# Batch norm over 64 tiles: loads and stores issued in turn from one ring of three buffers, in place of phases of three stores and three loads

## The chip, the cores and the metric

The kernel runs on one core of one Trainium2 chip. The metric is the device time of one execution in microseconds (us). A profiled execution also has a span, the time from its first to its last recorded event, which is about 1.8 us shorter. All runs named here are of the fast state; none fell into the slower state that some executions show. Where a ratio is given, it is the mean time of one kernel's fast runs over the mean of the other's fast runs of the same rounds, so it is not quite the ratio of the medians that stand beside it.

## The reference

```python
# x: (32, 256, 128, 128) float32; the parameters have 256 values, one for each channel
gamma * (x - running_mean) / np.sqrt(running_var + 1e-5) + beta
```

This is one multiplication and one addition for each element, with a scale and a shift that depend on the channel only. The input has 536.87 MB and so has the output. There is nothing to reuse, so the kernel is a stream: read everything, change it, write everything.

## The kernel before

The 32 x 256 channel planes are viewed as 64 tiles of 128 partitions by 16384 columns, 8.39 MB each, one contiguous row of 64 KB for each partition. Three such tiles fit the pool. All loads and stores go through the DMA queue of SP, the engine that issues them, in program order. DVE, the vector engine, does the arithmetic.

```python
NBUF = 3
GROUPS = [3] * 20 + [2, 2]
...
    def load(i):
        t = data.tile([P, HW], f32, tag="t")          # one of NBUF buffers in turn
        nc.sync.dma_start(out=t[:], in_=xr[i])
        tiles[i] = t
...
    def compute(i): ...                                # DVE, in place: t = t * scale + shift
    def store(i):
        t = tiles.pop(i)
        nc.sync.dma_start(out=outr[i], in_=t[:])
...
    first = 0
    for g, size in enumerate(GROUPS):
        idxs = range(first, first + size)
        for i in idxs:
            compute(i)
        for i in idxs:
            store(i)
        first += size
        more = GROUPS[g + 1] if g + 1 < len(GROUPS) else 0
        for i in range(first + AHEAD, min(first + AHEAD + more, NT)):   # AHEAD is 0
            load(i)
```

The framework puts in the waits: a compute waits for its load to land, a store for its compute, and a load for the store that frees its buffer.

## Time and profile before

| | before |
|---|---|
| time, median of the first 3 runs | 2487.11 us (2486.21 to 2487.93) |
| span of the profiled run | 2483.6 us |
| DVE busy | 566.0 us, 23% |
| share of the 16 DMA engines' time that the one data queue fills | 99.9% |
| mean rate | 432 GB/s |
| one load or store of a tile, in the steady part | 19.35 us |

The row to read first is the DMA engines' share. DVE is idle for three quarters of the span, but idle time of an engine that isn't the bound costs nothing. The lines themselves stand in the prediction.

### The profile page before, as it was taken

The numbers are of one execution on the slowest core, as the hardware profiler recorded it, in microseconds if no ns is written. First come the engines' busy times: TensorE is split into PE (matmuls) and PEld (weight loads), VectorE is DVE, ScalarE is ACT, GpSimd is POOL, SyncE is SP. The second block draws the span as 40 slices with busy tenths as digits, with TensorE's granted clock in tenths as the row PEclk, the third lists the DMA queues.
The fourth block names the chain that finished last, engine by engine and source line by source line (L and its number), as shares of the span: only waits on it lengthen the run. The fifth ranks groups of instructions, "written<-read, shape, count | busy, mean of one in ns | idle before, by whom it ended". The sixth has DMA issues, their size and how long they took to land.

```text
span 2483.6 us, 383 instructions
## 1 busy us (share of the span) xinstructions
DVE 566.0 (23%) x75; ACT 1.6 (0%) x2; POOL 0.2 (0%) x4
## 2 busy tenths in 40 slices
DVE  3140404121221213140403121221213040403112
ACT  0000000000000000000000000000000000000000
POOL 0000000000000000000000000000000000000000
DMA  9999999999999999999999999999999999999999
GB/s 421 423 439 439 425 436 439 431 431 439 431 431 439 435 426 436 436 431 435 435 435 427 439 434 427 439 434 427 439 437 432 432 437 433 431 437 433 431 437 396
DMA packets 18442, 1073.77 MB, mean 432 GB/s; under 512 B 2052, under 2 KB 2056, under 8 KB 2056
## 3 DMA queue, kind: packets, MB, share of 16 engines
q1 hardware_dynamic: 18432, 1073.75, 99.9%
q14 instruction: 2, 0.02, 0.0%
q10 hardware_dynamic: 8, 0.00, 0.0%
HBM read 536.88 MB, written 536.87 MB: 432 GB/s over the span
## 4 chain that ended last, share of the span: by engine, by line
another core or an unknown queue 72%; DVE 22%; DMA 4%; issue 0%; DVEq 0%; SPq 0%
DVE t L93 22%; DMA t<-in_x_dram 4%; DVEq L93 0%; SPq L51 0%; SPq L104 0%
## 5 line engine op out<-in xcount | busy, mean ns | idle before, releaser
L93 DVE TENSOR_SCALAR t<-t,scale_t,shift_t 128x16384 f32<-128x16384 f32 x64 | 564.0, 8812 | 1863.9 <-DMA t<-in_x_dram 1863.8
L66 DVE STREAM_TRANSPOSE turned<-rows 32x256 f32<-32x256 f32 x1 | 0.4, 432 | 21.5 <-DMA rows<-in_running_mean_dram 21.5
L78 ACT ACT_TABLE_LOAD x1 | 1.3, 1283 | 2.6 <-issue 2.6
L71 DVE COPY par<-turned 32x8 f32<-32x8 f32 x4 | 0.6, 161 | 0.1
L56 DVE MEMSET rows<- 32x256 f32 x1 | 0.3, 272 | 0.8 <-PEq L132 0.8
L78 ACT ACTIVATE tmp_t<-par,eps_t 128x2 f32<-128x2 f32 x1 | 0.3, 297 | 20.0 <-DVE par L71 20.0
L85 DVE RECIPROCAL tmp_t<-tmp_t 128x2 f32<-128x2 f32 x1 | 0.2, 165 | 0.4 <-ACT tmp_t L78 0.4
L87 DVE TENSOR_TENSOR tmp_t<-par,scale_t 128x2 f32<-128x2 f32 x1 | 0.2, 161 | 0.0
L88 DVE TENSOR_TENSOR shift_t<-par,tmp_t 128x2 f32<-128x2 f32 x1 | 0.2, 161 | 0.0
L86 DVE TENSOR_TENSOR scale_t<-par,tmp_t 128x2 f32<-128x2 f32 x1 | 0.2, 160 | 0.0
L132 POOL MEMSET const-uint8-127<- 128x1 uint8 x1 | 0.1, 103 | 0.0
L132 POOL MEMSET const-bfloat16-1.0<- 128x1 bf16 x1 | 0.1, 101 | 0.0
L132 POOL MEMSET const-float32-0.0<- 128x1 f32 x1 | 0.1, 98 | 0.2 <-issue 0.2
L132 POOL MEMSET const-float32-1.0<- 128x1 f32 x1 | 0.1, 98 | 0.0
L64 DVE MEMSET eps_t<- 128x1 f32 x1 | 0.1, 59 | 0.0
## 6 DMA issues: line engine op xcount, KB each, us to landing
t<-in_x_dram SPq DMA_DIRECT2D x64, 58.0
out_dram<-t SPq DMA_DIRECT2D x64, 49.1
rows<-in_running_var_dram ACTq DMA_DIRECT2D x1, 1.0 KB
rows<-in_gamma_dram ACTq DMA_DIRECT2D x1, 1.0 KB
rows<-in_beta_dram ACTq DMA_DIRECT2D x1, 1.0 KB
rows<-in_running_mean_dram ACTq DMA_DIRECT2D x1, 1.0 KB
```

The costliest lines, as they stand in the source:

```text
L56: nc.vector.memset(rows, 0.0)
L64: nc.vector.memset(eps_t, eps)
L66: nc.vector.transpose(out=turned[:], in_=rows[:])
L71: nc.vector.tensor_copy(out=par[q * B : (q + 1) * B], in_=blocks[:, :, q, 0:4])
L78: nc.scalar.activation(out=tmp_t[:], in_=var_t, func=mybir.ActivationFunctionType.Sqrt, bias=eps_t[:], scale=1.0,)
L85: nc.vector.reciprocal(out=tmp_t[:], in_=tmp_t[:])
L86: nc.vector.tensor_mul(out=scale_t[:], in0=gamma_t, in1=tmp_t[:])
L87: nc.vector.tensor_mul(out=tmp_t[:], in0=mean_t, in1=scale_t[:])
L88: nc.vector.tensor_sub(out=shift_t[:], in0=beta_t, in1=tmp_t[:])
L93: nc.vector.tensor_scalar(out=t[:], in0=t[:], scalar1=scale_t[:, cb : cb + 1], scalar2=shift_t[:, cb : cb + 1], op0=mybir.AluOpType.mult, ...
L132: nc = _bacc.Bacc("TRN2", target_bir_lowering=False, num_devices=1)
```

## The change

The phases go. After the first three loads, the queue gets one store and one load in turn. The intent of such a ring is a shorter wait of each load and store for its partner: each load is issued as soon as the one store that it depends on has landed. Below, "the ring" is the changed kernel and "the phases" the kernel before. A **switch** is a place in the order of transfers where a load is followed by a store. The queue runs dry when no issued transfer waits behind those in progress.

```diff
 NBUF = 3
-GROUPS = [3] * 20 + [2, 2]
-
-AHEAD = 0
@@
-    for i in range(AHEAD + GROUPS[0]):
+    for i in range(NBUF):
         load(i)
@@
-    first = 0
-    for g, size in enumerate(GROUPS):
-        idxs = range(first, first + size)
-        for i in idxs:
-            compute(i)
-        for i in idxs:
-            store(i)
-        first += size
-        more = GROUPS[g + 1] if g + 1 < len(GROUPS) else 0
-        for i in range(first + AHEAD, min(first + AHEAD + more, NT)):
-            load(i)
+    for i in range(NT):
+        compute(i)
+        store(i)
+        if 1 <= i and i + 2 < NT:
+            load(i + 2)
```

More of the change, by code (lines that the diff above doesn't have):

```diff
@@ L37 @@
     NQ = P // B
-    assert sum(GROUPS) == NT and max(GROUPS) <= NBUF
     params = ctx.enter_context(tc.tile_pool(name="params", bufs=1))
```

## The prediction

> **What bounds the kernel now.** I read the page first (busy shares, slices, queues), then the timeline of the first 260 us, then the waits of the DMA queue, then the issues. The page says that the sixteen DMA engines have no free time:
>
> ```profile
> span 2483.6 us, 383 instructions
> DVE 566.0 (23%) x75; ACT 1.6 (0%) x2; POOL 0.2 (0%) x4
> ...
> DMA  9999999999999999999999999999999999999999
> GB/s 421 423 439 439 425 436 439 431 431 439 431 431 439 435 426 436 436 431 435 435 435 427 439 434 427 439 434 427 439 437 432 432 437 433 431 437 433 431 437 396
> ...
> q1 hardware_dynamic: 18432, 1073.75, 99.9%
> HBM read 536.88 MB, written 536.87 MB: 432 GB/s over the span
> ```
>
> The reader is to see three things: DVE works 23% of the span; the one queue that carries all loads and stores keeps the engines at 99.9%; and the bytes are the least possible (64 tiles of 8.39 MB read once and written once). Nothing in the change alters the bytes. So only lost transfer time can be won or added.
>
> The timeline of one steady period of three tiles gives the unit of cost:
>
> ```profile
> 139.82 8.81 DVE L93 TENSOR_SCALAR t<-t,scale_t,shift_t 128x16384 f32<-128x16384 f32 x1 [68.58 <-DMA t<-in_x_dram]
> 148.66 39.13 SPq L104 DMA_DIRECT2D out_dram<-t  x3
> 159.22 8.81 DVE L93 TENSOR_SCALAR t<-t,scale_t,shift_t 128x16384 f32<-128x16384 f32 x1 [10.59 <-DMA t<-in_x_dram]
> 178.62 8.81 DVE L93 TENSOR_SCALAR t<-t,scale_t,shift_t 128x16384 f32<-128x16384 f32 x1 [10.58 <-DMA t<-in_x_dram]
> 197.85 39.28 SPq L51 DMA_DIRECT2D t<-in_x_dram  x3
> 255.91 8.81 DVE L93 TENSOR_SCALAR t<-t,scale_t,shift_t 128x16384 f32<-128x16384 f32 x1 [68.47 <-DMA t<-in_x_dram]
> ...
> 2231.36 8.81 DVE L93 TENSOR_SCALAR t<-t,scale_t,shift_t 128x16384 f32<-128x16384 f32 x1 [68.56 <-DMA t<-in_x_dram]
> ```
>
> Each DVE start follows the landing of a load by about 0.1 us. Two loads land 19.40 us apart, and from 178.62 to 255.91 three stores and one load pass in 77.29 us, 19.32 each. So a load and a store cost the same, **T = 19.35 us** (116.09 us for six transfers), and they run one behind another in the order of issue. The best periods of the trace are 116.07 us; over the 18 periods from 139.82 to 2231.36 the mean is 2091.54 / 18 = 116.20 us. The difference, **0.13 us a period**, is all that a steady period loses. It sits in one place: the other intervals between starts repeat near 19.35 and near 77.3, but the one between the second and the third load of a group is often longer (19.6 to 19.8, once 20.06; mean over groups 2 to 20 about 19.52). In the trace's packet records, too, the 64 KB packets take 2.418 us nearly all, and the longer ones gather in the last one or two packets of a load phase, just before the first store, at every group. None gather where stores give way to loads. I therefore book the 0.13 us to a load-to-store switch.
>
> The queue's own waits and the issues say how far ahead it is:
>
> ```profile
> SPq L104 <- DVE t L93: 1451.7, 64, 47.2
> SPq L51 <- DMA out_dram<-t: 950.3, 60, 19.3
> ...
> t<-in_x_dram SPq DMA_DIRECT2D x64, 58.0
> out_dram<-t SPq DMA_DIRECT2D x64, 49.1
> ```
>
> These long waits are of the issuing sequencer, not of the engines. A load takes 58.0 us from issue to landing, three times T: two transfers lie ahead of it when it is issued. A store takes 49.1, two and a half T. The engines therefore have about 30 to 39 us of queued work at each issue. 1451.7 us of waiting cost nothing as long as that stays so.
>
> **What the Trainium skill says.** "DMA: Bandwidth & Descriptors", section "Where 436 GB/s comes from", puts the ceiling of the sixteen ports at 435.2 GB/s. The trace agrees: 8.389 MB / 19.35 us = 433.6 GB/s, and 435 in the fastest whole-transfer stretches. Nothing above that is left to win. The same page, "Queues, rings and completion order", says that each engine consumes descriptors in ring order and that a later DMA may finish its write before an earlier one. The trace agrees as to order (the landings follow the issues), so the new issue order should be the new transfer order. "Perfetto Trace Analysis", section "What "DMA-bound" means", separates a bound on the engines from one on the issuing sequencer; here it is the engines, since one issue takes 0.34 us against T of 19.35. The pages I read give no cost for a switch between loads and stores in one ring, so that number can only come from this trace.
>
> **The change part by part.** The instructions are the same on every compute engine, and so are the 64 loads and 64 stores on the SP queue; only their order changes, from three loads and three stores in turn to L0 L1 L2 S0 S1 L3 S2 L4 S3 L5 and so on to L63 S62 S63. Three tile buffers remain.
>
> Removed: nothing. Compute, 64 x 8.81 us, stays beside the transfers.
>
> Waits: does the ring keep the engines fed? Load i+2 takes the buffer of tile i-1, so it waits for store i-1 to land. In the new order the ring then still holds load i+1 and store i, if store i has been issued. Store i waits for tile i's compute. Load i lands one T before store i-1 does, compute takes 8.81, so store i is issued about 9 us after load i's landing and 10 us before load i+2. So load i+2 is issued with 2T = 38.7 us queued and should take 3T = 58.0 us to land. Store i is issued behind half of store i-1 and all of load i+1: 2T - 9 = 30 us of work queued, about 49 us to landing. These are the margins of the kernel before. At the start the margin is once thinner (L3 is issued at the landing of S0 with only S1 ahead, one T), still far above the couple of microseconds that an issue takes to move data. At the end both kernels finish with two stores behind the last load, in the ring before that load has passed or soon enough: compute of 8.81 lies under S62's 19.35. Cost of waits: 0.
>
> Switches: before has 22 groups, so 22 load-to-store switches. The new order has one after L2 and one after each of the 61 loads L3 to L63: 62. Added: 40 x 0.13 = **5.2 us**. Store-to-load switches grow by 40 as well, at no cost that the trace shows.
>
> Sum: 2487.1 + 5.2 = 2492.3 us, **predicted 2492** us, a ratio of 1.002.
>
> **The rivals.**
> - *Nothing at all, 2487.* The 0.13 us may be a loss of a phase of several loads (engines drifting together or apart), not of the switch; then shorter phases may even shed it, at best 20 x 0.13 = 2.6 us: 2484. For it: in the first ten groups many switches cost hardly anything. Against it: the losses stand so exactly at the switch.
> - *A dear switch, 2500 to 2505.* The third interval exceeds T by about 0.17 us in the mean, and by 0.3 to 0.4 in many later groups; a switch inside a ring of single transfers might always cost that. 40 x 0.35 = 14 us: 2501. For it: the engines meet all switches nearly at once. Against: the periods, which count what is really lost, grow by only 0.13.
> - *A drained ring.* If the chain "store landed, load issued, first byte" lay open at each of 61 loads, with an estimated 2 us, it would be 122 us: 2609, slower by 5%. For it: three buffers are few and each load now waits for a store that landed just before. Against: the margin worked out above, of 30 us or more. It would need an ordering of the queue that I have misread.
> - *Mixed reads and writes disturb each other in HBM.* If both kinds in flight slowed every packet by 3%, 2560. Against: in the ring just one transfer is in progress at a time but for the short overlap at a boundary, and the packet times of loads and stores near boundaries are the same 2.418 us now, apart from the small loss counted.
>
> **Range and chances.** The middle is the floor plus 40 switches. The low end, 2484, is the first rival with switches that cost nothing; the high end, 2504, is the dear switch at 0.35 us plus 3 us of spread between runs (three runs before span 1.7 us). 2% is 50 us: gaining it would need 442 GB/s, above every ceiling seen, so faster gets 0.01. Slower by 2% needs one of the last two rivals; I give them 0.04 together. Within 2%: 0.95.
>
> **What would show it.** In the profile after: the DMA row all nines and q1 at 99.7% or more; DVE starts 38.7 to 38.9 us apart, with an idle of 29.9 us before each, in place of 10.6, 10.6 and 68.5; loads at 58 us and stores at 49 us to landing, as now. If the load's figure falls toward 20 to 40 us or the engines' share falls below 99%, the ring drains and my margin is wrong. If both figures grow beyond 59 and 50 with the engines still full, packets have become slower, and the mixing rival is right. If the spacing is 38.70 exactly, switches are free; at 39.05 they are dear.

## The result, and the profile after

The changed kernel took 2487.81 us (median of 4 runs, 2486.77 to 2491.25) beside 2487.14 us of the kernel before (4 runs), a ratio of 1.0005 with a 95% interval from 0.9988 to 1.0023. A second measurement with five rounds (below) gave 1.0004. The change does nothing that can be told from zero, and 2% is far away.

The page of the changed kernel has the same totals. DVE's row of slices shows the different order: an even 1 and 2 in place of bursts and pauses.

```profile
span 2486.6 us, 384 instructions
DVE 566.0 (23%) x75; ACT 1.6 (0%) x2; POOL 0.2 (0%) x4
...
DVE  3122121221212212122121221222212212122121
...
DMA  9999999999999999999999999999999999999998
...
q1 hardware_dynamic: 18432, 1073.75, 99.8%
HBM read 536.88 MB, written 536.87 MB: 432 GB/s over the span
```

The queue never ran dry: 99.8% in place of 99.9%, with the same packets and bytes. The timeline of the ring late in the run (start, duration, engine, line, instruction, and in brackets the idle time before it with its releaser) is:

```profile
2021.88 8.81 DVE L89 TENSOR_SCALAR t<-t,scale_t,shift_t 128x16384 f32<-128x16384 f32 x1 [29.88 <-DMA t<-in_x_dram]
2030.72 0.33 SPq L100 DMA_DIRECT2D out_dram<-t  x1
2041.13 0.34 SPq L47 DMA_DIRECT2D t<-in_x_dram  x1
2060.53 8.81 DVE L89 TENSOR_SCALAR t<-t,scale_t,shift_t 128x16384 f32<-128x16384 f32 x1 [29.84 <-DMA t<-in_x_dram]
```

One load and one store pass in 2060.53 - 2021.88 = 38.65 us, 19.33 each, a hair under the 19.35 of the phases. The store is issued as soon as its compute ends, and the next load 10.4 us later, when the previous store has landed. The waits of the queue and the times to landing of this kernel:

```profile
SPq L100 <- DVE t L89: 1765.2, 63, 38.2
SPq L47 <- DMA out_dram<-t: 640.3, 61, 30.8
...
t<-in_x_dram SPq DMA_DIRECT2D x64, 57.9
out_dram<-t SPq DMA_DIRECT2D x64, 49.0
```

The waits have moved from loads to stores (1451.7 and 950.3 before). Their sum is nearly the same, 2405.5 us against 2402.0. Loads land 57.9 us after issue and stores 49.0, against 58.0 and 49.1. The depth of queued work, which is what keeps the engines fed, didn't change.

What remains is the profiled span, 3.0 us longer. From the DVE start of the third tile to that of the last, during which 123 transfers pass in both kernels, it took 2446.99 - 62.51 = 2384.48 us after and 2443.92 - 62.43 = 2381.49 before, again 3.0. These are single executions: the profiled one of the kernel before took 2485.35 us, near the fast end of its runs, and that of the ring 2488.53, above the middle of its own. So 3.0 us is no more than runs of one kernel differ by; what the two traces look like inside says more. The starts after are 38.73 to 39.65 us apart in the first ten steady rounds and 38.60 to 38.70 from about 1000 us on. So the ring loses something early and nothing late, while the phases lose a little all the time.

The packet records in the trace show more of this. Each transfer ends on each of the 16 engines with a small completion packet. I call the time from the first to the last of these sixteen the **spread** of the engines, and I call the **loss** of a switch the time by which 64 KB packets near the end of its load exceed 2.418 us, summed and divided by 16. This table is worked out from those records; each row is a switch, and "landing" is when the first engines have finished its load:

```
kernel   landing us   spread us   loss us
before        61.8       0.70       1.22
before       177.8       0.70       0.11
before       525.8       1.16       0.08
before       873.9       2.07       0.34
before      1221.9       3.08       0.13
before      2149.8       4.29       0.15
after         61.9       0.57       1.19
after        120.2       0.75       0.19
after        313.5       2.75       0.24
after        545.4       5.73       0.21
after        815.9       7.77       0.18
after       1047.8       7.73       0.006
after       2129.9       7.77       0.012
```

In both kernels most of the lossy switches push the engines a little further apart. In the ring, with three times as many switches in the same time, the spread reaches 7.8 us by about 820 us and stays there, and from about 980 us on no switch loses 0.02 us or more. In the phases it creeps to 4.3 us, and switches go on costing. After the first switch, the packets of the ring lose 2.60 us an engine up to 905 us and 0.64 after that; those of the phases lose 0.98 and 1.59. So of the 3.0 us only some 0.8 are lost by the engines in the mean: they end their last transfer at 2480.09 us in the ring and at 2479.31 in the phases. The other 2.2 are the distance of the last engine behind this mean, 5.02 us beside 2.82, which grows with the spread. From the traces I formed a new theory: the loss limits itself, because engines that have drifted apart no longer switch together. It is tested below.

### The profile page after: what moved, and what is told of

Same layout as the page of the kernel before. It is cut to its first block, busy times and chain, and to the rows that moved or that the text cites. A ratio compares the mean times of both kernels' runs of the same rounds, so it can differ in the third digit from the quotient of the medians.

```text
span 2486.6 us, 384 instructions
## 1 busy us (share of the span) xinstructions
DVE 566.0 (23%) x75; ACT 1.6 (0%) x2; POOL 0.2 (0%) x4
## 3 DMA queue, kind: packets, MB, share of 16 engines
q1 hardware_dynamic: 18432, 1073.75, 99.8%
## 4 chain that ended last, share of the span: by engine, by line
another core or an unknown queue 72%; DVE 22%; DMA 4%; issue 0%; DVEq 0%; ACTq 0%; ACT 0%; SPq 0%
DVE t L89 22%; DMA out_dram<-t 2%; DMA t<-in_x_dram 2%; DMA rows<-in_running_mean_dram 1%; DVEq L89 0%; ACTq L54 0%; DVE par L67 0%; DVE turned L62 0%; ACT tmp_t L74 0%; DVE rows L52 0%; DVE tmp_t L81 0%; DVE shift_t L84 0%; DVE tmp_t L83 0%; DVE scale_t L82 0%
## 6 DMA issues: line engine op xcount, KB each, us to landing
t<-in_x_dram SPq DMA_DIRECT2D x64, 57.9
```

## The experiments

Theories: (A) the engines' own rate bounds both kernels, any order whose queue isn't dry is as good as another, and the switch loss dies away as the engines drift apart; (B) each switch has a fixed cost, as I predicted; (C) the depth of the queue matters by itself; (D) reads and writes in flight together disturb each other.

### Loads and stores on two queues

```diff
-        nc.sync.dma_start(out=outr[i], in_=t[:])
+        nc.scalar.dma_start(out=outr[i], in_=t[:])
```

> The ring of the changed kernel, with the stores issued from the ACT queue and the loads left on SP, so that the engines can take packets of loads and stores by turns. Theory (the engines' own rate bounds; a load-to-store switch costs only while many engines make it together, so the loss limits itself): 2484 to 2492 us, and 64 KB packets still at 2.418 us. Rival 1 (every change from load to store costs a fixed 0.13 us on an engine): with packets by turns there would be up to 8 changes a tile in place of one, 61 x 7 x 0.13 = 56 us more: about 2540 us. Rival 2 (reads and writes in flight together disturb each other in HBM by 3%): about 2560 us.

Measured: 2503.17 us (2502.11 to 2503.70), ratio 1.0069 (1.0054 to 1.0084). None of the three numbers was hit. The packet records show that loads and stores went by turns in the first part of the run: from 90 to 600 us, in 87% of the 211 steps from 16 packets to the next 16, most packets belong to the other queue. After 1000 us that falls to 23%; there most engines work on one queue for about six packets and then on the other. In the part with turns the mean 64 KB packet takes 2.421 us, beside 2.420 in the kernel before over the same time; over the whole run it is 2.426, and 95% take 2.418. So D's 3% is refuted. B's 56 us rested on turns throughout, which didn't last. In the part that had them an estimated 211 x 0.87 / 2 = 92 changes from load to store would by B have cost 12 us an engine; the packets lost 0.7. So B is refuted there too. Where are the 17 us? The windows view (window, its length, busy times, clock, DMA share, GB/s) of this run, and then of the kernel before:

```profile
100.00:2400.00 2300.00, 519.91 (x59) 0.00 (x0) 0.00 (x0) 1.00 1.00 433
2400.00:2450.00 50.00, 8.81 (x1) 0.00 (x0) 0.00 (x0) 1.00 1.00 434
2450.00:2501.60 51.60, 8.81 (x1) 0.00 (x0) 0.00 (x0) 1.00 0.62 268
```

```profile
100.00:2400.00 2300.00, 519.91 (x59) 0.00 (x0) 0.00 (x0) 1.00 1.00 434
2450.00:2483.60 33.60, 2.74 (x1) 0.00 (x0) 0.00 (x0) 1.00 0.83 361
```

The steady part is nearly the same, 433 against 434 GB/s. In the last window the engines stand idle for 0.38 x 51.6 = 19.6 us, against 0.17 x 33.6 = 5.7. Long packets add 8.6 - 4.4 = 4.2 us an engine. Together that is 18.1 us, and the spans differ by 18.0. With two queues, the last load and the store before it share the engines and end together; then the last compute of 8.81 us has nothing beside it, and the last store runs alone. At the end of that store one engine is also 4.2 us behind the other fifteen. In a single queue, that store passes while the last tile is computed. My expectation had overlooked the tail.

### A ring that runs dry

```diff
-NBUF = 3
+NBUF = 2
@@
-        if 1 <= i and i + 2 < NT:
+        if i + 2 < NT:
             load(i + 2)
```

> The ring with two buffers in place of three: load i+2 waits for store i, and store i+1 stands behind it in the queue, so the ring runs dry once for each load. Theory (three buffers are enough only because they keep about 30 us of work queued): each of some 62 gaps costs an estimated 2 us: about 2610 us, the engines' share near 95%, and DVE starts about 40.7 us apart. Rival (a load issued at the landing of a store is hidden anyway): 2484 to 2495 us.

Measured: 2721.52 us (2720.43 to 2722.68), ratio 1.0948 (1.0931 to 1.0964). Queue and timeline of this run:

```profile
q1 hardware_dynamic: 18432, 1073.75, 95.5%
...
128.47 8.81 DVE L89 TENSOR_SCALAR t<-t,scale_t,shift_t 128x16384 f32<-128x16384 f32 x1 [33.88 <-DMA t<-in_x_dram]
147.73 0.33 SPq L47 DMA_DIRECT2D t<-in_x_dram  x1
148.15 0.39 SPq L100 DMA_DIRECT2D out_dram<-t  x1
171.10 8.81 DVE L89 TENSOR_SCALAR t<-t,scale_t,shift_t 128x16384 f32<-128x16384 f32 x1 [33.81 <-DMA t<-in_x_dram]
```

The store is stuck behind a load that waits for the previous store, and both are issued together, into an empty queue. From the landing of the store to the first packet of the load it takes 1.3 us. A round takes 42.63 us in place of 38.65. The extra 235 us are 3.8 us for each of 62 gaps, about double what I estimated. Half of it is the gap: 4.5% of 2720.9 us, 122 us or 2.0 us each, which is what I had expected (the record doesn't say from what I had worked out that estimate). The other half is in the packets: they exceed 2.418 us by 120.5 us an engine in all. After each gap the first packets of the load are slow by 0.5 to 0.8 us, and the switch to the store that follows loses 1.1 to 1.5 us, at all 62 of them. Here the gap sets the engines back in step each time (the spread never passes 1.2 us), and the loss never dies away. Each switch then costs what the first switch costs in the other one-queue kernels that aren't pushed apart (1.1 to 1.3). So the drained ring is a real and dear danger, and the changed kernel doesn't have it.

### Phases with two buffers

```diff
-NBUF = 3
-GROUPS = [3] * 20 + [2, 2]
+NBUF = 2
+GROUPS = [2] * 32
```

> The kernel before with two buffers and groups of two. A store is issued about 9 us after its tile's load has landed, with the group's other load (19.35 us) still in the ring: a margin of about 10 us in place of 30. Theory (any margin[...] is as good as a large one): 2485 to 2492 us, ratio 0.999 to 1.002. Rival (depth of the ring matters by itself): above 2500 us.

Measured: 2486.15 us (2486.07 to 2486.53), ratio 1.0001 (0.9984 to 1.0017). The times to landing in this run:

```profile
t<-in_x_dram SPq DMA_DIRECT2D x64, 38.6
out_dram<-t SPq DMA_DIRECT2D x64, 29.7
```

Each is one transfer shorter than with three buffers, so the margin is about 10 us, and the time is the same. C is refuted from 10 us of queued work up. The switches of this run lose 0.00 to 0.29 us after the first (1.10), but one, at a spread of 3.2 us, loses 0.74. The same two buffers in ring order cost 9.5%.

### One switch in the whole run

Its output is wrong, which doesn't matter for the time.

```diff
-    for i in range(NT):
-        compute(i)
-        store(i)
-        if 1 <= i and i + 2 < NT:
-            load(i + 2)
+    for i in range(NBUF):
+        compute(i)
+    for i in range(NT):
+        nc.sync.dma_start(out=outr[i], in_=tiles[i % NBUF][:])
+    for i in range(NBUF, NT):
+        load(i)
+        if i + 1 < NT:
+            compute(i)
```

> Wrong result on purpose: three loads, then all 64 stores from these three tiles, then the other 61 loads. The same 128 transfers and bytes, with one load-to-store switch in place of 22 or 62. It measures the floor. Theory: 128 x 19.345 = 2476.2 us, plus 1.2 us at the first switch and about 3 us of head and tail: a span near 2480.5 and a time near 2484 us, 3 us under the kernel before, and the spread of the sixteen engines' landings stays under 1 us to the end. If the spread grows all the same, switches aren't what drives the engines apart. If the time is 2487 or more, the switches weren't what cost the difference from the floor.

Measured: 2485.45 us (2485.35 to 2486.09), ratio 0.9998 (0.9984 to 1.0013): no gain that can be told from zero, where I expected 3 us. Part of the expectation holds: the spread is 0.8 us at first and 0.5 at the end of the stores. It grows to 1.0 at the change from stores to loads and to 1.7 at about 1700 us, where there is no switch at all; so switches drive the engines apart, but not they alone. And the floor is not lower. The first 40 stores land 19.32 us apart; but from about 900 us on stores, and later most loads, land 19.36 apart, as two neighbouring DVE starts of this run show (2405.91 - 2386.55 = 19.36 us):

```profile
2386.55 8.81 DVE L89 TENSOR_SCALAR t<-t,scale_t,shift_t 128x16384 f32<-128x16384 f32 x1 [10.56 <-DMA t<-in_x_dram]
...
2405.91 8.81 DVE L89 TENSOR_SCALAR t<-t,scale_t,shift_t 128x16384 f32<-128x16384 f32 x1 [10.54 <-DMA t<-in_x_dram]
```

So long runs of one kind, with the engines nearly in step, lose about 0.04 us a transfer, some 3 us over the 80 or so of them; why it starts there is open. There was also a loss of 1.1 us at the change from stores to loads: 0.8 on the last packets of the store and 0.3 on the first of the load. The queue wasn't dry there, for the loads are issued from 1280.87 us on, the last store landed at 1300.5, and its engines went on to the load without a gap:

```profile
1280.87 68.70 SPq L47 DMA_DIRECT2D t<-in_x_dram  x4
```

What the switches don't take, the long runs and this one change do.

### Twice as many switches

```diff
-NBUF = 3
+NBUF = 6
@@
-    NT = N * NCB
+    NT = N * NCB * 2
+    HALF = HW // 2                     # tiles of HALF columns; load, store and channel block follow
@@
-        if 1 <= i and i + 2 < NT:
-            load(i + 2)
+        if 1 <= i and i + 5 < NT:
+            load(i + 5)
```

> The ring with tiles of half the columns and six buffers: the same bytes and the same amount queued, 126 load-to-store switches in place of 62. Fixed cost (my prediction's 0.13 us a switch): 64 x 0.13 = 8.3 us more than the ring, about 2496 us; at the 0.35 us of the dear rival 2510 us. Theory now (the losses die away as the sixteen engines drift apart, whatever the number of switches): 2485 to 2491 us, with the losses all in the first part of the run and the spread of the engines' landings settling at several us.

Measured: 2492.17 us (2491.78 to 2492.57), ratio 1.0024 (1.0010 to 1.0037), 5.5 us more than the kernel before. It lies just outside A's range and 4 us under B's. The late timeline of this run shows what kind of cost it is:

```profile
2034.46 4.55 DVE L90 TENSOR_SCALAR t<-t,scale_t,shift_t 128x8192 f32<-128x8192 f32 x1 [14.86 <-DMA t<-in_x_dram]
2053.84 4.55 DVE L90 TENSOR_SCALAR t<-t,scale_t,shift_t 128x8192 f32<-128x8192 f32 x1 [14.83 <-DMA t<-in_x_dram]
2073.17 4.55 DVE L90 TENSOR_SCALAR t<-t,scale_t,shift_t 128x8192 f32<-128x8192 f32 x1 [14.78 <-DMA t<-in_x_dram]
```

From about 500 us on, the starts are 19.37 us apart in the mean, against half of 38.65, which is 19.33. The 32 KB packets take 1.213 us, 4 ns more than half of 2.418, so with 32 of them in a load and a store of a whole tile the smaller packets cost something all the time. The uneven intervals (19.4 to 20.3 us) mostly stop at about 400 us, sooner than in the ring of whole tiles, and the spread settles at 5.6 us. (The kernel as built has 123 switches, not the 126 that I had counted.) A second set of some 60 switches didn't bring a second set of losses: between the first switch and 500 us the packets exceed 1.213 us by 2.4 us an engine, beside 2.6 in the ring of whole tiles up to 905. The packet size did the rest. The total alone wouldn't have told A from B.

### Engines pushed apart from the start

Five small loads after the first, which are overwritten later, hand some of the engines more work than the others. The same edit was made to the ring and to the kernel before.

```diff
-        nc.scalar.dma_start(out=rows[r : r + 1, :], in_=...)      # parameters
+        nc.sync.dma_start(out=rows[r : r + 1, :], in_=...)
@@
-    for i in range(NBUF):
+    pad = data.tile([P, HW], f32, tag="t")
+    PADF = 10240
+    load(0)
+    for s, j in enumerate((2, 5, 8, 11, 14)):
+        nc.sync.dma_start(out=pad[16 * s : 16 * s + j, 0:PADF], in_=xr[s][0:j, 0:PADF])
+    for i in range(1, NBUF):
         load(i)
```

> The ring with the engines pushed apart on purpose: after the first load, five small loads of 2, 5, 8, 11 and 14 rows of 40 KB into a buffer that is overwritten later, so that the engines start their second tile in steps of about 1.5 us, 7.5 us from first to last (the small parameter loads are put ahead on the same queue, some 1.7 us). If the drift itself ends the losses, the ring from the second switch on shows under 0.05 us of loss a switch where the changed kernel shows 0.03 to 0.24 in its first twenty, the spread stays near 7.5 to 8.5 us from the start, and the time is that of the ring plus 0 to 4 us (2487 to 2492), because the lead of the spread is paid once either way. If the losses go on for the first twenty switches as before, spread isn't what ends them, the spread grows to some 15 us and the time is about 2497 us.

> The same push given to the kernel before. Spread theory: its 20 later switches, which lose 0.13 us a period in the kernel before, lose under 0.05 each; the spread starts near 7.5 us and grows by less than 1; 2486 to 2491 us. Otherwise the spread grows by 3.5 us as in the kernel before, to 11, and the time is about 2494 us.

Measured: 2503.98 us (2503.74 to 2504.47) for the ring and 2504.07 us (2503.97 to 2504.47) for the phases. Both totals missed. The push itself was dearer than I reckoned: a row of 40 KB took 3.1 to 5.3 us on the engines that had one, not 1.5, and the third load had to wait for these loads, so the third compute began at 85.46 us in place of 62.51. That is a cost of 23 us ahead of the part that the experiment is about. The steady part answers the question. It is the time from the third DVE start to the last, with the same 123 transfers in each kernel:

```
kernel                  third   last      difference   span
before                  62.43   2443.92   2381.49      2483.6
ring                    62.51   2446.99   2384.48      2486.6
ring, second run        63.26   2447.45   2384.19      2487.1
ring, pushed apart      85.46   2462.24   2376.78      2502.0
phases, pushed apart    85.40   2462.51   2377.11      2502.3
```

Pushed apart, the ring's steady part is 7.7 us shorter and the phases' 4.4, and the two then agree to 0.3 us. The ring's DVE starts are 38.60 to 38.70 us apart from the fourth tile on, with no uneven start, save one pair at about 900 us. From the packet records: the first switch of the ring loses 0.03 us in place of 1.19, each of the next twenty loses 0.012 or less, and the spread stays at 9.3 us. In the phases the switches lose about 0.04 each up to 830 us, and the spread is 9.0 us at first and 7.9 at the end. So spread engines do end the switch loss, also at a first switch, and with that loss gone the two orders cost the same. Not all of the 7.7 us is lost packet time: after the first switch the packets of the pushed ring lose 0.8 us an engine in place of 3.2. Most of the rest is that the last engine was already behind the mean when this stretch began. It doesn't make a faster kernel, because the lead of the early engines is itself time in which the late ones still work: what could be saved is the 2.4 us of packet time, 0.1%.

### The changed kernel again

No edit.

> The changed kernel again, with five rounds, to size a difference under 1%. Prediction of a fixed cost: ratio 1.002 (5 us). Self-limiting loss: 1.0003 to 1.0012 (1 to 3 us), as the first look had it (1.0005).

Measured: 2487.42 us (2486.01 to 2488.92), beside 2486.64 of the kernel before, ratio 1.0004 (0.9991 to 1.0016). This interval leaves out B's 1.002; the first one, with fewer runs, had just held it. The profiled execution, 2488.92 us, was the slowest of the five. Its trace repeats the first one: a spread growing to 8.5 us by about 860 us, and level starts of 38.60 to 38.71 from 925 us on.

## Why the prediction was right or wrong

The time lay inside the range and the call of "within 2%" was right: 2492 predicted, 2487.8 and 2487.4 measured.

*What bounds the kernel.* Right. The engines were 99.8% busy in the new order, with packets of the same duration. No order of the same transfers tried here had a median below 2485 us; the one-switch kernel is the nearest to a floor that was measured. The slices of 439 GB/s in the page that I showed don't contradict the ceiling: 439 GB/s over a slice of 62.1 us would be 26.0 packets of 64 KB an engine, which take 26 x 2.418 = 62.9 us, so such a slice counts a packet that isn't wholly in it.

*The waits of the ring.* Right, and to the tenth: 57.9 and 49.0 us to landing against a forecast of 58.0 and 49. The margin argument was tested from both sides. Ten us of queued work still cost nothing (two buffers in phases), while none at all costs 3.8 us a round (two buffers in a ring). The drained ring was therefore rightly named as a rival that could have made the change slow, although its cost was put at 2 us a gap; that is the idle part alone. (The trace of the kernel before has 1.0 us from its first issue, at 0.73, to its first packet, at 1.74.)

*The switches.* This step failed in size. I booked 0.13 us to each load-to-store switch, "40 x 0.13 = 5.2 us". The loss does stand at that switch in the phases, but it isn't a constant. It was 1.1 to 1.5 us where an idle queue came just before, at most 0.34 while the engines of the two kernels drift apart, and under 0.02 in the ring from about 980 us on, at a spread near 8 us. Forty more switches made the engines reach that point sooner, and the packets lost 3.2 us an engine after the first switch in place of 2.6. The profiled span grew by 3.0 us, most of it the last engine's distance behind the mean, and the timed runs by 0.7 and 0.8 us, which their own scatter covers. My average over the phases had mixed switches at different spreads and then extended it to a kernel that spends most of its time at another spread.

The 0.13 itself was read against a wrong floor. I called 116.07 us the best periods, but four of these 18 are shorter, down to 115.90. With the 38.65 us that a load and a store take late in the ring as the floor, a switch costs 116.20 - 115.95 = 0.25 us in the phases, and in the ring, whose starts from the fourth tile on are (2446.99 - 120.91) / 60 = 38.77 us apart in the mean, 0.12. The two kernels don't share one cost of a switch. That 0.13 is near what the packet records of the phases give (2.57 us over 21 later switches, 0.12) is luck.

*The rivals.* "Nothing at all, 2487" came closest in the number. Its reason, engines that drift together or apart, was named but not followed up, and its expected gain of up to 2.6 us didn't come. The dear switch is real after an idle queue, and now and then elsewhere (0.74 us once in the phases with two buffers), but not as a rule. Mixed reads and writes were refuted by the two queues: 2.421 beside 2.420 us on the mean packet where they alternate.

What stays open: why a switch costs anything when engines make it together, and what beside the spread decides how much. The second switch of the kernel before lost only 0.11 us at the same spread as the first, which lost 1.22 in the first round after an idle queue. An idle queue isn't needed for such a loss either: the change from stores to loads in the one-switch run lost 1.1 us with work queued, at a spread of 0.5. What the runs show is one direction: engines pushed 9 us apart lose next to nothing at any switch.

## What to carry to other kernels

When one queue keeps the DMA engines at 99.9% with the least possible bytes, don't expect a gain from reordering the transfers: none of the orders tried here had one that can be told from zero, and two lost. Ask of a new order two things: at the moment when each transfer is issued, is there still work queued ahead of it, and do the last compute and the last store have something beside them? Here 10 us of queued work were as good as 30, so two buffers in phases do the work of three, while two buffers in this ring lose 9.5%. And don't multiply a small average loss by a count before you know whether it is the same at every event.

## What the Trainium skill lacked or had wrong

- "DMA: Bandwidth & Descriptors", section "Latency and other measured facts" and the measured tables: no cost of a change between loads and stores in one queue. The runs show 1.1 to 1.5 us at a load-to-store switch soon after an idle queue, mostly under 0.35 us (0.74 once) with whole tiles while the engines are within some 8 us of each other, and under 0.02 us in the ring after 980 us, at a spread of about 8 us.
- "DMA: Bandwidth & Descriptors", section "Why a DMA increments its semaphore by 16 and not by 1", says that the engines finish independently, but not that they can drift apart and stay so. The runs show a spread of 0.6 to 0.7 us growing to 4.3 us (phases) and 7.8 us (ring), where it stands still from about 820 us on.
- "DMA: Bandwidth & Descriptors", section "Anatomy of one DMA — SWDGE (gpsimd) path", has a fixed time for a single DMA on a path that isn't used here, but no page that I read tells what a dry queue costs in a stream of them. The runs show 3.8 us for each gap: 2.0 us idle, the rest in slower packets just after it and at the next switch.
- "DMA: Bandwidth & Descriptors", section "Issuing engines are not separate DMA queues", holds for bandwidth (433 against 434 GB/s in the steady part), but a reader might conclude that the choice of queue is free. Here the second queue cost 17 us, of which some 14 were idle time at the tail.
